# A third weights tile, two plain blocks instead of three in three of the four feed-forward layers, and earlier weight requests in sparse attention

## The chip, the cores and the metric

The kernel runs on one core of one Trainium2 chip, as one launch. The metric is the device time of that launch in microseconds (us). The median of three runs of the kernel before is 1895.46 us (1894.83 to 1896.32).

## What is computed

Two layers of a decoder on 512 tokens of width 1024, all float32. Each layer is a feed-forward part (ffn), a token mixer, and a second ffn, and every part has an RMS norm ahead of it. The mixer of the first layer is multi-head latent attention (mla, 16 heads), that of the second is native sparse attention (nsa, 16 heads in 4 groups; a compressed, a selected and a window branch with gates). So there are four ffns, numbered 0 to 3 in the code (`idx`).

```python
def swiglu(x, w_gate, w_up, w_down):
    return (jax.nn.silu(x @ w_gate) * (x @ w_up)) @ w_down
...
for i in range(DEPTH):
    h = h + 0.5 * swiglu(rmsnorm(h, ffn_norm_a[i]), ...)
    m = rmsnorm(h, mix_norm[i])
    ...
    h = h + 0.5 * swiglu(rmsnorm(h, ffn_norm_b[i]), ...)
return rmsnorm(h, final_norm)
```

The hidden width of an ffn is 2816, worked in 22 blocks of 128.

## The kernel before, in words

**Number format.** Every weight and activation is split into a high and a low part (`hi` is a rounded copy made by ScalarE, ACT; `lo` is the rest, a subtraction on VectorE, DVE, or on GpSimd, POOL). A product is three matmuls on TensorE (PE): high by high, high by low, low by high (`mm3`, L163 to L165).

**An ffn.** The residual `h` stands in eight tiles of 128 x 512. Of the 22 hidden blocks, the first three (`PLAIN`) are plain (L365 to L367): gate and up, each 8 chunks by 2 token halves by 3 matmuls of 256 columns, 96 in a block. A plain block needs only the split of `h`, chunk by chunk as the residual gets done. The other 19 blocks use Strassen's scheme with seven products (L353 to L355): 7 by 4 by 3, that is 84 matmuls of 256 columns. For that, sums of the weights (`wsums`, DVE and ACT) and sums of the activations (`combine`, made once in an ffn, for four pairs of chunks) are needed first. Besides, the blocks from the second of each three on carry `unit`s: the down projection of three finished blocks, one output chunk in each (9 matmuls of 512 columns). The last four blocks' down projection comes at the ffn's end.

**The norm's factor of ffns 1 to 3.** After the first plain block the column of sums of squares is finished (`norm_col`, four small matmuls `pc` on PE, then twelve small DVE operations, L260 to L272), then spread over the partitions by PE (`norm_bcast`, `pb`, L291) and copied to `row` by ACT. With `row` the gate of each plain block is formed (`gate`, `act`: three DVE steps of 512 columns, a Silu on ACT, and a split). Before, `pb` is written between the gate and the up half of the third plain block.

**Weight tiles.** `wslab` (L133) asks a slab of 128 x 1024 from memory (SyncE's queue) into one of two raw buffers `wr`, and splits it into a weights tile `w`. Two such tiles alternate (`wtiles`, tags w0 and w1). The plain blocks, the mixers and a part of each Strassen block (`w[1]`, `w[2]` of `wsums`, split from `rg` at L172) use them. A tile is written anew only when the matmuls that read it are done.

**Sparse attention.** `attend` goes through 96 tiles (24 in each of 4 groups): scores on PE, softmax on DVE and ACT, a scaling of the probabilities on POOL (`p`, L1091), a transpose on PE four tiles later, and the product with the values. `todo` hangs other work to tile numbers: the query, key and value projections of the next group (`make`, `vals`) and a part of the output projection (`w_o`). The first piece of each projection asks for its weights and uses them at once. While `lo_pool` is set, the low half of weights is made on POOL in two steps (L150). `compressed(g)` is done in three steps: scores, softmax (whose last step is on POOL, `e`, L1053) and `turn`, four transposes of `e` on PE (`ptc`, L1058).

**Order.** The kernel is written in program order, and the framework sets the order of each engine's queue by its own cost model and priorities. Within an engine's queue the work goes in that order, and a waiting instruction holds the ones behind it.

## Time and profile before

| | |
|---|---|
| median of the three runs | 1895.46 us |
| the profiled execution: its time | 1895.84 us |
| the profiled execution: its span | 1894.1 us |
| DVE busy | 1527.9 us (81%) |
| ACT busy | 1088.9 us (57%) |
| POOL busy | 244.7 us (13%), in the two mixers alone |
| memory | 97 GB/s mean |

How to read it: the span goes from the first to the last instruction of the profiled execution, and its own time has 1.7 us more. The ends of matmuls are modelled, so the busy time of PE overlaps itself; what a matmul costs is read from the distance between the starts of two that follow each other. The number behind the bar in a row of instructions is the time in which the engine stood idle before that group, and behind the arrow stands who ended it.

### The profile page before, as it was taken

The numbers are of one execution on the slowest core, as the hardware profiler recorded it, in microseconds if no ns is written. First come the engines' busy times: TensorE is split into PE (matmuls) and PEld (weight loads), VectorE is DVE, ScalarE is ACT, GpSimd is POOL, SyncE is SP. The second block draws the span as 40 slices with busy tenths as digits, with TensorE's granted clock in tenths as the row PEclk, the third lists the DMA queues.
The fourth block names the chain that finished last, engine by engine and source line by source line (L and its number), as shares of the span: only waits on it lengthen the run. The fifth ranks groups of instructions, "written<-read, shape, count | busy, mean of one in ns | idle before, by whom it ended". The sixth has DMA issues, their size and how long they took to land.

```text
span 1894.1 us, 32916 instructions
## 1 busy us (share of the span) xinstructions
PE 1865.5 (98%) x12504; PEld 1695.8 (90%) x12504; DVE 1527.9 (81%) x2913; ACT 1088.9 (57%) x2024; POOL 244.7 (13%) x334
## 2 busy tenths in 40 slices
PE   8999999999999999999999999999989999999998
PEld 8999999878889999998999999888778889999997
DVE  8988886677778888886898878666978988888885
ACT  8555554478765555554654555436867865555553
POOL 0000000047710000000000000015656600000000
PEclk9999999999999999999999999999999999999999
DMA  6433331311132333322333332143121133333321
GB/s 237 131 101 100 102 100 41 112 53 46 60 132 90 124 101 101 102 79 86 130 124 108 105 105 75 55 141 102 51 71 64 43 115 111 111 107 104 104 77 67
DMA packets 75902, 183.26 MB, mean 97 GB/s; under 512 B 9040, under 2 KB 37072, under 8 KB 75744
## 3 DMA queue, kind: packets, MB, share of 16 engines
q1 hardware_dynamic: 72800, 176.39, 29.4%
q10 hardware_dynamic: 2944, 4.77, 0.7%
q8 instruction: 98, 1.61, 0.4%
q14 instruction: 60, 0.49, 0.1%
HBM read 178.96 MB, written 2.16 MB: 96 GB/s over the span
## 4 chain that ended last, share of the span: by engine, by line
PE 86%; DVE 6%; ACT 4%; POOL 2%; issue 1%; DMA 0%; POOLq 0%; SPq 0%; DVEq 0%; ACTq 0%
PE pd L164 8%; PE pd L165 8%; PE pd L163 8%; PE px L353 5%; PE px L354 5%; PE px L355 5%; PE pg L353 4%; PE pg L354 4%; PE pg L355 4%; PE pq L354 3%; PE pq L353 3%; PE pq L355 3%; PE o L1139 1%; PE po L164 1%; PE po L165 1%; PE po L163 1%
## 5 line engine op out<-in xcount | busy, mean ns | idle before, releaser
L164 PE MATMUL pd<-al,wd 128*128 128x512 f32 x576 | 225.3, 391 | 0.0
L163 PE MATMUL pd<-ah,wd 128*128 128x512 f32 x576 | 224.9, 390 | 0.0
L165 PE MATMUL pd<-ah,wd 128*128 128x512 f32 x576 | 224.6, 390 | 0.0
L172 DVE TENSOR_TENSOR w<-wr,w 128x1024 fp32r<-128x1024 f32 x72 | 88.2, 1224 | 123.9 <-ACT w L171 123.9
L353 PE MATMUL px<-four,wh 128*128 128x256 f32 x608 | 168.8, 278 | 0.6 <-ACT pg L478 0.6
L355 PE MATMUL px<-four,wl 128*128 128x256 f32 x608 | 168.0, 276 | 0.0
L354 PE MATMUL px<-four,wh 128*128 128x256 f32 x608 | 167.9, 276 | 0.0
L353 PE MATMUL pq<-four,wh 128*128 128x256 f32 x608 | 167.8, 276 | 0.0
L354 PE MATMUL pq<-four,wh 128*128 128x256 f32 x608 | 167.8, 276 | 0.0
L355 PE MATMUL pq<-four,wl 128*128 128x256 f32 x608 | 167.8, 276 | 0.0
L144 ACT ACTIVATE w<-wr 128x1024 fp32r<-128x1024 f32 (+5 forms) x120 | 100.7, 845 | 113.7 <-issue 25.7
L171 ACT ACTIVATE wd<-wdr 128x384 fp32r<-128x384 f32 x192 | 99.3, 519 | 98.5 <-ACT wd L171 59.1
L402 DVE SCALAR_TENSOR_TENSOR h<-pd,h 128x512 f32<-128x512 f32 x216 | 147.9, 685 | 6.9 <-PE pd L165 6.8
L165 PEld LDWEIGHTS pd<-ah,wd 128*128 128x128 f32 x576 | 108.2, 188 | 22.8
L163 PEld LDWEIGHTS pd<-ah,wd 128*128 128x128 f32 x576 | 108.1, 188 | 20.5
L164 PEld LDWEIGHTS pd<-al,wd 128*128 128x128 f32 x576 | 108.1, 188 | 19.7
L172 DVE TENSOR_TENSOR wd<-wdr,wd 128x384 fp32r<-128x384 f32 x192 | 106.1, 555 | 16.3 <-ACT wd L171 15.6
L146 DVE TENSOR_TENSOR w<-wr,w 128x1024 fp32r<-128x1024 f32 (+4 forms) x81 | 80.7, 998 | 45.1 <-ACT w L144 44.8
L640 ACT ACTIVATE p<-p,small 128x512 f32<-128x512 f32 (+2 forms) x192 | 106.5, 557 | 17.2 <-DVE small L639 14.2
L353 PEld LDWEIGHTS px<-four,wh 128*128 128x128 f32 x608 | 114.1, 188 | 2.5 <-ACT pg L478 1.9
L353 PEld LDWEIGHTS pq<-four,wh 128*128 128x128 f32 x608 | 114.2, 188 | 0.1
L354 PEld LDWEIGHTS pq<-four,wh 128*128 128x128 f32 x608 | 114.1, 188 | 0.1
(354 smaller groups left out, 6106.3 us busy)
## 6 DMA issues: line engine op xcount, KB each, us to landing
wr<-in_w_gu SPq DMA_DIRECT2D x96, 512.0 KB, 3.3
ru<-in_w_gu SPq DMA_DIRECT2D x76, 512.0 KB, 4.2
wdr<-in_w_down SPq DMA_DIRECT2D x192, 192.0 KB, 2.4
wr<-in_w_down SPq DMA_DIRECT2D x24, 256.0 KB, 2.6
wr<-in_mla_w_o SPq DMA_DIRECT2D x8, 512.0 KB, 3.4
wr<-in_nsa_w_q SPq DMA_DIRECT2D x8, 512.0 KB, 3.3
th<-btab_d SPq DMA_DIRECT2D x16, 256.0 KB, 3.5
wr<-in_nsa_w_o SPq DMA_DIRECT2D x8, 512.0 KB, 3.6
```

The costliest lines, as they stand in the source:

```text
L144: self.copied = nc.scalar.activation(wh[:, m], raw[:, m], AF.Copy)
L146: nc.vector.tensor_tensor(wl[:, m], raw[:, m], f32v(wh[:, m]), op=ALU.subtract)
L163: mm(out, wh, xh, start=first, stop=False)
L164: mm(out, wh, xl, start=False, stop=False)
L165: return mm(out, wl, xh, start=False, stop=last)
L171: nc.scalar.activation(hi, src, AF.Copy)
L172: (nc.gpsimd if pool else nc.vector).tensor_tensor(lo, src, f32v(hi), op=ALU.subtract)
L353: mm(out, wh[:, p], xh, start=first and p == 0, stop=False, skip_group_check=True)
L354: mm(out, wh[:, p], xl, start=False, stop=False, skip_group_check=True)
L355: mm(out, wl[:, p], xh, start=False, stop=last and p == KP - 1, skip_group_check=True)
L402: nc.vector.scalar_tensor_tensor(self.h[c], p, 0.5, self.h[c], op0=ALU.mult, op1=ALU.add)
L640: nc.scalar.activation(p_sb[:, :n], p_sb[:, :n], AF.Exp, bias=nm, scale=-1.0, accum_out=sm)
```

## The change

- `PLAIN` becomes a tuple: three plain blocks in ffn 0, two in ffns 1, 2 and 3. So one more block in each of three ffns is a Strassen block. `pb` and the gates (`spread`) now stand between the gate and the up half of the last plain block, the second one in ffns 1 to 3. The sums `combine` go behind the first and the second block.
- `norm_col`'s DVE operations, and the last sums of squares ahead of them, get a higher priority (400) in ffns 1 to 3.
- `wtiles` takes turns among three tiles; the third starts with 80 unused columns, so that all tiles behind it keep their address modulo 512 bytes. 15 KB of another reservation are given up for it.
- The down projection of the last four blocks no longer uses weight tiles and `wr`, but the buffers of the Strassen sums (`fr`, `fh`, `fl`).
- In sparse attention the request for weights (`load`) is an entry of its own, one to four tiles ahead of the first piece. `turn` of groups 1 to 3 goes from 21 or 22 to 25, that is to the second tile of the next group. The scratch `t` of queries and keys gets a second buffer, and `ot` a buffer of its own.
- Latent attention: the low half of the first two queries in flight (heads 0 and 1) and of the last output go from POOL to DVE.

```diff
-PLAIN = 3
+PLAIN = 3, 2, 2, 2
...
-        t = self.first or self.wp.tile([P, 2048 + 3 * PAD], F32R, tag=f"w{self.nw % 2}", name="w")
+        shift = 5 * PAD if self.nw % 3 == 2 else 0
+        t = self.first or self.wp.tile([P, 2048 + 3 * PAD + shift], F32R, tag=f"w{self.nw % 3}", name="w")[:, shift:]
...
-        return self.rsqrt_col(pc[:, 0:4], n, pool)
+        with self.tc.high_priority(urgent) if urgent else nullcontext():
+            return self.rsqrt_col(pc[:, 0:4], n)
...
+        def spread():
+            pb = self.norm_bcast(col)
+            nc.scalar.activation(row, pb, AF.Copy)
+            for e in range(plain - 1):
+                gate(e, gates[e])
+                act(e)
...
             self.plain(idx, f, 0, g)
+            if f == plain - 1:
+                spread()
...
-            for p in (((0,), (1,), (2, 3)) if idx else ((0, 1), (2,), (3,)))[f]:
+            for p in (((0, 1), (2, 3)) if plain == 2 else ((0, 1), (2,), (3,)))[f]:
                 self.combine(p)
...
-        for f in range(PLAIN, NF):
+        for f in range(plain, NF):
...
-            down(p, self.wslab(a["w_down"][idx, c, :, tail * P :], (NF - tail, P), "act"), tail, NF)
+            raw = tp.tile([P, D], F32, tag="fr", bufs=3, name="wdr")[:, : (NF - tail) * P]
+            nc.sync.dma_start(raw, a["w_down"][idx, c, :, tail * P :])
+            w = [t[:, : (NF - tail) * P].rearrange("p (k c) -> p k c", c=P) for t in self.sum_tiles(1024)]
+            self.split(raw.rearrange("p (k c) -> p k c", c=P), *w)
+            down(p, w, tail, NF)
...
-                self.split(t, qh, ql, pool=True)
+                self.split(t, qh, ql, pool=h > 1)
...
-                    self.split(o32[0], hi, lo, pool=True)
+                    self.split(o32[0], hi, lo, pool=h + 1 < H)
...
-                return [partial(piece, k0) for k0 in range(0, KC, KC // nk)] + more
+                return [load] + [partial(piece, k0) for k0 in range(0, KC, KC // nk)] + more
...
-            make(2, (0, 1, 3, 4, 5, 6), (4, 5, 7, 8, 9, 10), (9, 10, 11, 12, 13, 14), (16, 18, 21))
-            at(2, vals(), 12, 13, 14, 15, 16, 17, 19, 20)
+            make(2, (-2, 0, 1, 3, 4, 5, 6), (2, 4, 5, 7, 8, 9, 10), (6, 9, 10, 11, 12, 13, 14), (16, 18, 25))
+            at(2, vals(), 9, 11, 12, 13, 14, 15, 16, 17, 19, 20)
```

Three places in the queues. First PE in ffn 2, before, at the norm's spread (`pb`); `pg_10244` is the gate of the third plain block.

```order
L366 MATMUL pg_10244<-x_10231,w_10504 128x256
L367 MATMUL pg_10244<-x_10231,w_10504 128x256
L365 MATMUL pg_10244<-x_10231,w_10504 128x256
L366 MATMUL pg_10244<-x_10231,w_10504 128x256
L367 MATMUL pg_10244<-x_10231,w_10504 128x256
L291 MATMUL pb_10556<-ident_79,small_76 128x128 x4
```

The same place after; `pu_10420` is the up half of the second plain block, and its lines are L368 to L370 now.

```order
L368 MATMUL pu_10420<-x_10207,w_10491 128x256
L369 MATMUL pu_10420<-x_10207,w_10491 128x256
L294 MATMUL pb_10474<-ident_79,small_76 128x128 x4
L370 MATMUL pu_10420<-x_10207,w_10491 128x256
L368 MATMUL pu_10420<-x_10233,w_10491 128x256
```

`pb` stood behind three gates and two up halves; now it stands behind two gates, one up half and 35 of the 48 matmuls of the second up half. In ffn 1 it is 21 of the 48 and in ffn 3 it is 29.

Second, DVE in ffn 2, before: the end of the norm's small operations (`small`), the weights of the last plain block (`w_10504`, `w_10584`), and the first split of the first Strassen block (`w_10674<-rg`).

```order
L146 TENSOR_TENSOR w_10504<-wr_10503,w_10504 128x1024
L271 TENSOR_TENSOR small_76<-small_76 128x4
L172 TENSOR_TENSOR wd_10810<-wdr_10811,wd_10809 128x384
L272 SCALAR_TENSOR_TENSOR small_76<-small_76 128x4
L172 TENSOR_TENSOR wd_10827<-wdr_10828,wd_10826 128x384
L146 TENSOR_TENSOR w_10584<-wr_10583,w_10584 128x1024
L172 TENSOR_TENSOR w_10674<-rg_10669,w_10674 128x1024
L378 TENSOR_TENSOR tg_10563<-pg_10242,row_10561 128x512
```

The same engine and ffn after, in two stretches: the first split of the first Strassen block (`w_10580<-rg`) among the small operations, and then their end, with the weight sums of the second Strassen block (`s1_10707`, `ru_10705`) behind it.

```order
L263 TENSOR_SCALAR small_76<-small_76 128x4
L240 TENSOR_TENSOR u_10564<-y_10563,u_10564 128x256
L264 TENSOR_SCALAR small_76<-small_76 128x4
L174 TENSOR_TENSOR w_10580<-rg_10575,w_10580 128x1024
...
L274 SCALAR_TENSOR_TENSOR small_76<-small_76 128x4
L342 TENSOR_TENSOR s1_10707<-ru_10705 128x512
L174 TENSOR_TENSOR wd_10827<-wdr_10828,wd_10826 128x384
L343 TENSOR_TENSOR ru_10705<-ru_10705,wr_10703 128x512
L174 TENSOR_TENSOR wl_10592<-rg_10575,wh_10591 128x1024
L381 TENSOR_TENSOR tg_10480<-pg_10268,row_10267 128x512
```

The split that closed the plain stage now stands in the middle of the norm's operations, and the sums of a further block begin ahead of the gates.

Third, POOL in sparse attention, before: the low half of the second value slab (`w_15658`) between the scalings `p`.

```order
L150 TENSOR_TENSOR w_15652<-wr_15651,w_15652 128x512 x2
L1091 TENSOR_SCALAR p_15508<-p_15508,small_76,gat_14124 128x512
L1091 TENSOR_SCALAR p_15532<-p_15532,small_76,gat_14124 128x512
L1091 TENSOR_SCALAR p_15564<-p_15564,small_76,gat_14124 128x384
L1091 TENSOR_SCALAR p_15604<-p_15604,small_76,gat_14124 128x384
L1091 TENSOR_SCALAR p_15626<-p_15626,small_76,gat_14124 128x256 x2
L150 TENSOR_TENSOR w_15658<-wr_15657,w_15658 128x512 x2
```

After, the second value slab is `w_15670`, and `w_16013` is the first query slab of group 3.

```order
L152 TENSOR_TENSOR w_15670<-wr_15669,w_15670 128x512 x2
L1105 TENSOR_SCALAR p_15556<-p_15556,small_76,gat_14166 128x512
L1105 TENSOR_SCALAR p_15580<-p_15580,small_76,gat_14166 128x512
L1105 TENSOR_SCALAR p_15612<-p_15612,small_76,gat_14166 128x384
L1105 TENSOR_SCALAR p_15652<-p_15652,small_76,gat_14166 128x384
L1105 TENSOR_SCALAR p_15680<-p_15680,small_76,gat_14166 128x256 x2
L152 TENSOR_TENSOR w_16013<-wr_16012,w_16013 128x512 x2
```

Each slab's low half stands one slab earlier among the same scalings.

More of the change, by code (lines that the diff above doesn't have):

```diff
@@ L49 @@
 KP = KC // 2
-PLAIN = 3
+PLAIN = 3, 2, 2, 2
 PAD = 16
+URGENT = 400
 TILES = 24
@@ L371, in ffn @@
         self.scr, self.fp = (tp, "sq", 1), tp
-        ah, al, ht, row = {}, {}, [], None
+        ah, al, ht, plain = {}, {}, [], PLAIN[idx]
         tg, tu, units = {}, {}, []
@@ L386, in act @@
             t = tu[f]
-            if f < PLAIN:
+            if f < plain:
                 t = tu_tile()
@@ L427, in ffn @@
                 tokens(t)
-        gates = [self.bank("T", "pg") for _ in range(PLAIN)]
+        def spread():
[4 more added lines that the diff above has]
+                act(e)
+        row = tp.tile([P, S], F32, tag="row", bufs=1, name="row")
+        gates = [self.bank("T", "pg") for _ in range(plain)]
         for f, g in enumerate(gates):
@@ L438, in ffn @@
                 squares(1)
-            if f == 2:
-                pb = self.norm_bcast(col)
-                row = tp.tile([P, S], F32, tag="row", bufs=1, name="row")
-                nc.scalar.activation(row, pb, AF.Copy)
-                for e in range(2):
-                    gate(e, gates[e])
-                    act(e)
             self.plain(idx, f, 1, u)
             if f == 0 and idx:
-                for c in self.late:
-                    self.sumsq(self.h[c])
-                col = self.norm_col(D, self.s2)
+                with self.tc.high_priority(URGENT):
+                    for c in self.late:
+                        self.sumsq(self.h[c])
+                col = self.norm_col(D, self.s2, URGENT)
             elif f == 1 and idx == 0:
@@ L462, in ffn @@
             nc.scalar.activation(t[:, i + 1 : i + 2], g[:, 0:1], AF.Identity, bias=t[:, i : i + 1])
-        tail = PLAIN + (NF - 2 - PLAIN) // NG * NG
-        for f in range(PLAIN, NF):
+        tail, left = (NF - 2) // NG * NG, 1
+        for f in range(plain, NF):
             if f % NG == 0 and f <= tail:
@@ L857, in pieces, with load @@
                 p, w = [], []
+                def load():
+                    w.extend(self.wslab(src, (KC, P)))
                 def piece(k0):
                     if k0 == 0:
-                        w.extend(self.wslab(src, (KC, P)))
                         p.append(self.mm_bank("pp"))
@@ L874, in done @@
                 def done(p):
-                    tt.append(qp.tile([P, S], F32, tag="t", bufs=1, name="t"))
+                    tt.append(qp.tile([P, S], F32, tag="t", bufs=2, name="t"))
                     nc.vector.tensor_tensor(tt[0], p, row, op=ALU.mult)
@@ L901, in vals, with load @@
                 ws = []
+                def load(z):
+                    ws.append(self.wslab(a["nsa_w_v"][z], (4, 256), "half"))
                 def piece(j, kk):
-                    if not ws:
-                        ws.extend(self.wslab(a["nsa_w_v"][z], (4, 256), "half") for z in range(2))
                     if kk == 0:
@@ L914, in piece @@
                         values(1, j, p)
-                return [partial(piece, j, kk) for j in range(4) for kk in range(2)]
+                return [partial(load, z) for z in range(2)] + [partial(piece, j, kk) for j in range(4) for kk in range(2)]
             def query(t2):
@@ L921, in done @@
                 def done(p):
-                    tt.append(qp.tile([P, S], F32, tag="t", bufs=1, name="t"))
+                    tt.append(qp.tile([P, S], F32, tag="t", bufs=2, name="t"))
                     nc.vector.scalar_tensor_tensor(tt[0], p, 0.125, row, op0=ALU.mult, op1=ALU.mult)
@@ L984, in nsa @@
                 kf = keys(0)
-                for f in kf[:2]:
+                for f in kf[:3]:
                     f()
@@ L991, in nsa @@
                 self.split(pk[:, : G * 32].rearrange("p (g n) -> p g n", g=G), at(kch), at(kcl))
-                for f in kf[2:]:
+                for f in kf[3:]:
                     f()
@@ L1173, in w_o, with load @@
                 w = []
+                def load():
+                    w.append(self.wslab(a["nsa_w_o"][0, c2], (2, 4, P), "act"))
                 def piece(e):
-                    if e == 0:
-                        w.append(self.wslab(a["nsa_w_o"][0, c2], (2, 4, P), "act"))
                     self.w_o1(w[0], oh[:4], ol[:4], c2 + KP * e, e, False)
-                return [partial(piece, e) for e in range(2)]
+                return [load] + [partial(piece, e) for e in range(2)]
             todo = {}
```

18 lines of the change are left out of this document (9 added, 9 removed).

## Prediction

> **What bounds the kernel now.** I read the page's busy times and chain first, then PE's waits, and then the timelines of the places that the change touches.
>
> ```profile
> PE 1865.5 (98%) x12504; PEld 1695.8 (90%) x12504; DVE 1527.9 (81%) x2913; ACT 1088.9 (57%) x2024; POOL 244.7 (13%) x334
> PE 86%; DVE 6%; ACT 4%; POOL 2%; issue 1%; DMA 0%; POOLq 0%; SPq 0%; DVEq 0%; ACTq 0%
> ```
>
> PE is busy for 98% of the span and carries 86% of the chain that ended last. So there are two ways to gain: fewer matmuls, or fewer of PE's few waits. These are the longest but for the kernel's start (engine, line, who ended it: us in total, times, longest):
>
> ```profile
> PE ptc L1058 <- POOL e L1053: 4.1, 4, 2.4
> PE pv L164 <- POOL w L150: 1.7, 2, 1.0
> PE pg L353 <- ACT pg L485: 1.2, 3, 0.8
> PE pv L163 <- ACT w L144: 0.7, 1, 0.7
> PE s L165 <- POOL four L172: 0.6, 1, 0.6
> PE po L164 <- POOL ol L172: 0.6, 1, 0.6
> PE pp L165 <- POOL w L150: 0.6, 1, 0.6
> PE px L353 <- ACT pg L478: 0.6, 3, 0.2
> ```
>
> All of them are touched by the change. I give each part its own price, as a change of the profiled execution's time of 1895.84 us (0.38 above the median of the runs shown).
>
> **A. Fewer matmuls.** Three plain blocks of 96 matmuls become Strassen blocks of 84: 36 fewer, all of 128 x 256. Their real price is the distance of starts, not the 276 ns of the page. In a steady Strassen block, the second product's first matmul and the last product's last one, 71 starts apart:
>
> ```profile
> 1131.37 0.28 PE L353 MATMUL pq<-four,wh 128*128 128x256 f32 x1
> ...
> 1139.41 0.28 PE L355 MATMUL pg<-x,wl 128*128 128x256 f32 x1
> ```
>
> That is 8.04 / 71 = 0.1133 us each, and 36 of them are **-4.1 us**. PE is the bound in this stage, so they count in full if nothing comes late.
>
> **B. The third tile at the ffns' openings.** ACT copied the first Strassen block's `rg` only when PE had released a weights tile, and DVE idled behind it in ffn 2:
>
> ```profile
> 926.95 1.06 ACT L171 ACTIVATE w<-rg 128x1024 fp32r<-128x1024 f32 x1 [4.33 <-PE pg L367]
> ```
> ```profile
> 922.65 1.23 DVE L146 TENSOR_TENSOR w<-wr,w 128x1024 fp32r<-128x1024 f32 x1 [1.44 <-ACT w L144]
> 928.04 1.22 DVE L172 TENSOR_TENSOR w<-rg,w 128x1024 fp32r<-128x1024 f32 x1 [4.16 <-ACT w L171]
> ```
>
> With a third tile these copies go ahead. PE's own waits from such late copies are those of `pg` (1.2) and `px` (0.6); between 0 and -1.8 I take **-1.0**, as new ones of the kind may come.
>
> **C. The norm's spread comes earlier than its factor.** This speaks against the change. In ffn 2 the new place of `pb` is 48 + 35 matmuls behind `pc`, which ends at 910.32:
>
> ```profile
> 909.51 0.95 PE L279 MATMUL pc<-ones,s 128*128 128x1 f32 x8
> 910.32 0.36 PE L365 MATMUL pg<-x,w 128*128 128x256 f32 x1
> ```
>
> So PE would be there at 910.32 + 83 x 0.1133 = 919.72; before, 144 matmuls stood between. DVE's twelve small operations ran from 911.30 on, with long ones in between, to the last of them:
>
> ```profile
> 905.08 0.69 DVE L237 TENSOR_TENSOR u<-y 128x512 f32<-128x512 f32 x1
> 905.68 0.42 DVE L239 TENSOR_TENSOR u<-y,u 128x256 f32<-128x256 f32 x1
> 906.02 0.42 DVE L238 TENSOR_TENSOR u<-y,u 128x256 f32<-128x256 f32 x1
> 906.35 1.22 DVE L172 TENSOR_TENSOR four<-u,four 128x1024 fp32r<-128x1024 f32 x1
> 907.49 1.22 DVE L146 TENSOR_TENSOR w<-wr,w 128x1024 fp32r<-128x1024 f32 x1
> ...
> 911.30 0.15 DVE L260 TENSOR_SCALAR small<-pc 128x4 f32<-128x4 f32 x1
> 911.37 1.21 DVE L172 TENSOR_TENSOR four<-u,four 128x1024 fp32r<-128x1024 f32 x1
> ...
> 920.59 0.15 DVE L272 SCALAR_TENSOR_TENSOR small<-small 128x4 f32<-128x4 f32 x1
> ```
>
> The rows give DVE's steps: 1.14 for 1024 columns, 0.60 for 512, 0.34 for 256, 0.07 for a small one. In the new order five of 1024, four of 512 and two of 256 stand between the twelve: 5.7 + 2.4 + 0.68 + 0.84 = 9.6, an end at 920.9, and PE waits 1.2. In ffns 1 and 3 the same sum starts from
>
> ```profile
> 572.59 0.36 PE L365 MATMUL pg<-x,w 128*128 128x256 f32 x1
> 1554.76 0.36 PE L365 MATMUL pg<-x,w 128*128 128x256 f32 x1
> ```
> ```profile
> 572.95 0.16 DVE L260 TENSOR_SCALAR small<-pc 128x4 f32<-128x4 f32 x1
> 1555.28 0.15 DVE L260 TENSOR_SCALAR small<-pc 128x4 f32<-128x4 f32 x1
> ```
>
> with 69 and 77 matmuls ahead of `pb` (PE there at 580.41 and 1563.48) and 8.0 and 8.8 us of DVE order (ffn 1: three of 1024, four each of 512 and 256; ffn 3: four, four, three): ends at 580.97 and 1564.10, waits of 0.6 and 0.6. Together **+2.4**. Behind the waiting `pb` stand the rest of the up half and the whole Strassen block, so PE pays each wait in full. The bounds are 0, if DVE gets there a little sooner, and 5, if each is some 0.8 later.
>
> Is the rest of DVE's work in time? In ffn 2 its new order from the last residual add to the low half of the block's second sums (needed by the third product) has sixteen operations of about 512 columns, nine of 1024, eight of 256 and twelve small: 9.6 + 10.3 + 2.7 + 0.8 = 23.4.
>
> ```profile
> 899.27 0.68 DVE L402 SCALAR_TENSOR_TENSOR h<-pd,h 128x512 f32<-128x512 f32 x1
> ```
>
> From 899.27 that is 922.7. PE begins the block at 910.32 + 96 x 0.1133 + 0.8 (`pb`) + 1.2 = 923.2 and its third product 24 matmuls later, at 925.9: 3.2 us to spare. I cost it at nothing, and the cover is these 3.2 us.
>
> **D. `turn` four tiles later.** The four waits on `e` sum to 4.1; that of group 0 stays, at 0.36. The longest one:
>
> ```profile
> 1315.00 0.33 PE L1058 MATMUL ptc<-ident,e 128*128 128x128 f32 x1 [0.36 <-POOL e L1053]
> 1411.34 0.66 PE L1058 MATMUL ptc<-ident,e 128*128 128x128 f32 x4 [2.38 <-POOL e L1053]
> ```
>
> At most -3.7. The turned tile is first read at the group's tile 10 (the first end, 3, and the lead and lag of 4 and 3), so at tile 1 it is still in time.
>
> **E. Weights asked early.** `pv` and `pp` waited 1.7 + 0.7 + 0.6 = 3.0 for slabs. And just behind the `pv` waits, PE's granted clock fell (window, length, PE, PEld, DVE, ACT, POOL busy, then PEclk):
>
> ```profile
> 1382.00:1387.00 5.00, 2.54 (x14) 1.90 (x13) 3.90 (x12) 4.09 (x10) 4.26 (x5) 0.91 0.05 17
> 1387.00:1389.00 2.00, 2.00 (x11) 2.00 (x11) 1.28 (x7) 0.42 (x2) 1.37 (x2) 0.50 0.78 262
> 1389.00:1395.00 6.00, 6.00 (x44) 5.58 (x44) 2.43 (x14) 3.08 (x12) 1.46 (x4) 0.96 0.01 3
> ```
>
> 5 x 0.09 + 2 x 0.50 + 6 x 0.04 = 1.7 us of clock lost, right after the stretch in which PE was busy for 2.54 of 5 us. I count it to the same waits: at most -4.7. [...] After the wait of 2.38 us the clock did not fall (the 0.99 of the 120 us below is this one fall, 1.7 of 120), so the trace does not settle it.
>
> The request passes SyncE's table loads, ACT's exponentials and POOL's scalings by one to four tiles, and on POOL it holds them for
>
> ```profile
> 1371.44 2.58 POOL L150 TENSOR_TENSOR w<-wr,w 128x512 fp32r<-128x512 f32 x2
> ```
>
> 2.58 us, as it did in its old place; the probabilities have a lead of four tiles to cover it. I add nothing.
>
> D and E make -8.4 at most. I take three quarters, **-6.3**: in that stage DVE is busy for 98.81 of 120 us, and a softmax that is behind can take a freed wait over.
>
> ```profile
> 1300.00:1420.00 120.00, 112.68 (x647) 94.17 (x646) 98.81 (x318) 93.69 (x235) 78.04 (x105) 0.99 0.24 74
> ```
>
> **F. Latent attention's three low halves on DVE.** PE's waits for POOL there are 0.6 (`s`) and 0.6 (`po`); a 512-column step of DVE takes 0.60. **-1.0** (0 to -1.2). The ffns' last down weights keep their operations and only change buffers: 0.
>
> **G. Matmuls that read the third tile.** No row shows it. The nearest are the two products that read weights tiles:
>
> ```profile
> L354 PE MATMUL px<-x,w 128*128 128x256 f32 x304 | 85.3, 281 | 0.0
> L354 PE MATMUL pg<-x,w 128*128 128x256 f32 x304 | 83.9, 276 | 0.0
> ```
>
> 24 of a block's 84 matmuls read such a tile, in 79 blocks every third time the new one: 632, and 5 ns each way are 3.2 us. Its address is the same modulo 512 as the others', so I take **0**.
>
> **Sum.** -4.1 - 1.0 + 2.4 - 6.3 - 1.0 + 0 = -10.0 against 1895.84, so 1885.8, and 1885.5 on the scale of the median.
>
> **Rivals.**
> - *All goes well*: no new wait and every old one gone, -4.1 - 1.8 - 8.4 - 1.2 = -15.5: 1880.0. For it: `pb`'s lateness is under a microsecond in two ffns. Against: DVE's load in sparse attention. 0.13.
> - *The clock falls anyway*, as a mechanism of its own: three quarters of 1.7 stay: 1886.8. 0.10.
> - *The waits only move*, that is, the early requests don't do what they say, because there are still two raw buffers and one POOL queue, and the softmax takes the waits over: A, B and C alone, -2.7: 1892.8. For it: POOL 78.04 and DVE 98.81 of 120 us. Against: the low halves stand one slab earlier in POOL's queue. 0.13.
> - *Slower: DVE becomes the bound of the openings.* If DVE ends the first Strassen split no sooner than before (928.04 + 1.22 = 929.26), PE, there at 923.2, waits 6.1 in each of three ffns: +18.2, and -10.0 + 18.2 = +8.2: 1903.7. It decides from 3.3 us an ffn. For it: DVE was busy for 27.40 of 33 us there. Against: the new order has that split among the norm's operations, and the tile it needs is free. 0.06.
>
> ```profile
> 900.00:933.00 33.00, 33.00 (x294) 33.00 (x293) 27.40 (x51) 19.20 (x27) 0.00 (x0) 1.00 0.47 158
> ```
>
> **How the numbers follow.** The forecast has 0.58. Within 0.2% of 1895.46 (3.8 us, about what a measurement of this kernel tells from no change) lie most of the "waits only move" case: same 0.10. Slower 0.06, faster 0.84. The range reaches from the best case, 1880.0, up to 1891.5; left out are most of "waits only move" and the slower case, 0.19 together. It holds C's bounds (1883.1 to 1888.1), and D, E together from the full gain to about 0.
>
> **What would show it.** In the profile after: 36 fewer matmuls; PE's waits for `e` down to about 0.4 and for `w` in sparse attention gone; no clock of 0.50 near the value projection; a wait of `pb` for `small` of about 1 us in each of ffns 1 to 3; no idle of DVE behind `w<-rg`. I am wrong if PE waits several us at the first or second Strassen block, or if the sparse attention stage is no shorter.

## The result, and the profile after

The changed kernel takes 1883.27 us (median of four runs, 1882.53 to 1884.34), the kernel before 1895.74 us on the same chip: a ratio of 0.9935, 95% interval 0.9918 to 0.9952. The prediction was 1885.5 us. The profiled execution after has a span of 1882.5 us and a time of 1884.34 us, 11.5 us less than the one before.

The page after: busy times, and the chain that ended last.

```profile
PE 1859.2 (99%) x12468; PEld 1691.9 (90%) x12468; DVE 1550.1 (82%) x2940; ACT 1080.1 (57%) x2039; POOL 243.2 (13%) x331
PE 85%; DVE 7%; ACT 4%; DMA 2%; issue 1%; POOL 0%; SPq 0%; DVEq 0%; ACTq 0%; POOLq 0%
```

The 36 matmuls are gone (12504 to 12468). PE's waits after (us in total, times, longest):

```profile
PE pb L294 <- DVE small L274: 1.9, 4, 0.9
PE s L165 <- DVE small L650: 1.6, 4, 0.7
PE px L356 <- ACT pg L485: 1.1, 3, 0.5
PE pg L356 <- ACT pg L492: 0.6, 3, 0.3
PE s L167 <- DVE four L174: 0.5, 1, 0.5
PE ptc L1072 <- POOL e L1067: 0.4, 1, 0.4
```

All waits for `w` in sparse attention are gone, and `ptc` is down from 4.1 to 0.4. New or longer are `pb` (0.2 before) and, in mla, `s` for DVE's `small` (0.2 before) and `four` (0.6 for POOL's before). `px` and `pg` together are 1.7, as against 1.8 before: they have moved, not gone.

Where did the time come from? Both traces are cut at PE's first matmul of each stage. Lengths in us:

| stage | before | after | difference |
|---|---|---|---|
| ffn 0 | 340.39 | 340.75 | +0.36 |
| mla | 214.72 | 214.96 | +0.24 |
| ffn 1 | 337.66 | 337.63 | -0.03 |
| ffn 2 | 337.32 | 337.45 | +0.13 |
| nsa | 307.23 | 297.31 | -9.91 |
| ffn 3 | 342.91 | 340.62 | -2.29 |

So sparse attention gave nearly all, and ffns 1 and 2 gave nothing although each lost 12 matmuls. The order of ffn 0 is the same in after and in e2, e3, e5, e7, e8 and e11 below, and its length went from 340.57 to 343.64 us over these executions, so no difference under 3 us is read from that stage. Ffns 1 and 2 have the same order in after, e2, e3 and e5 and took 336.88 to 337.68 and 336.87 to 337.76 us, so that tenths there are read from waits, not from lengths.

The stretch of sparse attention whose row the prediction showed, after (length, then PE, PEld, DVE, ACT, POOL busy, PEclk):

```profile
1300.00:1420.00 120.00, 118.51 (x692) 99.73 (x691) 105.33 (x345) 100.52 (x256) 83.84 (x114) 1.00 0.24 77
```

PE is busy for 118.51 us of 120, where it was 112.68, and the clock is full throughout. DVE went from 98.81 to 105.33 and did not become the bound.

What took the gain of ffns 1 and 2? First the new `pb`. The timeline after, DVE, in ffn 1:

```profile
573.36 0.16 DVE L262 TENSOR_SCALAR small<-pc 128x4 f32<-128x4 f32 x1 [0.52 <-PE pc L281]
...
575.33 1.22 DVE L174 TENSOR_TENSOR w<-rg,w 128x1024 fp32r<-128x1024 f32 x1
576.47 0.16 DVE L274 SCALAR_TENSOR_TENSOR small<-small 128x4 f32<-128x4 f32 x1
...
581.38 0.15 DVE L274 SCALAR_TENSOR_TENSOR small<-small 128x4 f32<-128x4 f32 x1
```

Twelve small operations of 0.16 us take 8.2 us, because the order puts up to 1.22 us of other work between each two. PE waits 0.40, 0.36 and 0.24 us for the last of them in ffns 1 to 3. Second, waits in the middle of the ffns. ACT, after, at a place of ffn 1:

```profile
856.34 1.06 ACT L146 ACTIVATE w<-wr 128x1024 fp32r<-128x1024 f32 x1 [2.47 <-DMA wr<-in_w_gu]
857.31 0.36 ACT L492 ACTIVATE pg<-px 128x256 f32<-128x256 f32 x1
```

A weights tile is free, so ACT's queue has come to the copy of the next slab; but there are only two raw buffers, the slab is still on its way, and ACT stands for 2.47 us with the product's copy behind it. PE waits 0.20 us for that copy. With 0.16 us more for each matmul that starts again after a wait (this one stands 0.47 us behind the one before it, 0.20 of that the wait, where others of its kind are 0.11 apart), 12 matmuls less and the waits that went and came make -0.3 us in ffn 1, -0.4 in ffn 2 and -2.6 in ffn 3. Measured are 0.0, +0.1 and -2.3, so 0.3 to 0.5 us in each stay unexplained.

The groups of ACT's copies of `rg` slabs show the same for the whole kernel (busy us, mean ns, then the idle time ahead of them and who ended it), before and after:

```profile
L171 ACT ACTIVATE w<-wr 128x1024 fp32r<-128x1024 f32 x72 | 76.5, 1062 | 60.5 <-PE pg L355 58.8 <-DMA wr<-in_w_gu 1.7
```
```profile
L173 ACT ACTIVATE w<-wr 128x1024 fp32r<-128x1024 f32 x75 | 78.7, 1049 | 6.9 <-DMA wr<-in_w_gu 6.6 <-PE pg L370 0.2
```

Before, ACT waited 58.8 us for PE to release a tile and 1.7 for the DMA. After, the wait for PE is gone and that for the DMA is 6.6.

In mla, `pb` (the query norm's) waits 0.91 us where it was 0.24. All engines, after:

```profile
396.16 1.03 POOL L152 TENSOR_TENSOR w<-wr,w 128x384 fp32r<-128x384 f32 x1 [6.16 <-ACT w L146]
...
396.33 0.87 DVE L272 SCALAR_TENSOR_TENSOR small<-small 128x4 f32<-128x4 f32 x1
...
397.75 0.46 PE L294 MATMUL pb<-ident,small 128*128 128x128 f32 x2 [0.91 <-DVE small L274]
```

One small operation takes 0.87 us, its neighbours 0.16, and it ends (397.20) when POOL's subtraction ends (397.19). With a third tile this slab is split earlier than before, beside the norm (with two tiles, in e1, no small operation is stretched, and `pb` waits 0.27 us).

### The profile page after: what moved, and what is told of

Read it like the earlier page. It is cut to its first block, busy times and chain, and to the rows that moved or that the text cites. A ratio compares the mean times of both kernels' runs of the same rounds, so it can differ in the third digit from the quotient of the medians.

```text
span 1882.5 us, 32808 instructions
## 1 busy us (share of the span) xinstructions
PE 1859.2 (99%) x12468; PEld 1691.9 (90%) x12468; DVE 1550.1 (82%) x2940; ACT 1080.1 (57%) x2039; POOL 243.2 (13%) x331
## 4 chain that ended last, share of the span: by engine, by line
PE 85%; DVE 7%; ACT 4%; DMA 2%; issue 1%; POOL 0%; SPq 0%; DVEq 0%; ACTq 0%; POOLq 0%
PE pd L166 8%; PE pd L165 8%; PE pd L167 8%; PE px L356 5%; PE px L357 5%; PE px L358 5%; PE pg L356 4%; PE pg L357 4%; PE pg L358 4%; PE pq L357 3%; PE pq L358 3%; PE pq L356 3%; PE o L1153 2%; PE pt L1128 2%; PE po L165 2%; PE po L167 2%
## 5 line engine op out<-in xcount | busy, mean ns | idle before, releaser
L356 PE MATMUL px<-four,wh 128*128 128x256 f32 x632 | 175.4, 278 | 1.2 <-ACT pg L485 1.1
L357 PE MATMUL px<-four,wh 128*128 128x256 f32 x632 | 174.6, 276 | 0.0
L358 PE MATMUL pq<-four,wl 128*128 128x256 f32 x632 | 174.4, 276 | 0.0
L356 PE MATMUL pq<-four,wh 128*128 128x256 f32 x632 | 174.4, 276 | 0.0
L357 PE MATMUL pq<-four,wh 128*128 128x256 f32 x632 | 174.4, 276 | 0.0
L174 DVE TENSOR_TENSOR wl<-s,wh 128x512 fp32r<-128x512 f32 x79 | 54.5, 690 | 123.0 <-ACT wh L173 122.9
L146 ACT ACTIVATE w<-wr 128x1024 fp32r<-128x1024 f32 (+5 forms) x90 | 79.2, 888 | 87.0 <-PE po L167 17.5
L173 ACT ACTIVATE wh<-s 128x512 fp32r<-128x512 f32 x79 | 49.8, 630 | 134.5 <-PE px L357 131.0
L356 PEld LDWEIGHTS px<-four,wh 128*128 128x128 f32 x632 | 118.6, 188 | 2.6 <-ACT pg L485 2.4
L358 PEld LDWEIGHTS pq<-four,wl 128*128 128x128 f32 x632 | 118.7, 188 | 0.0
L357 PEld LDWEIGHTS px<-four,wh 128*128 128x128 f32 x632 | 118.7, 188 | 0.0
L358 PEld LDWEIGHTS px<-four,wl 128*128 128x128 f32 x632 | 118.6, 188 | 0.0
L356 PEld LDWEIGHTS pq<-four,wh 128*128 128x128 f32 x632 | 118.6, 188 | 0.0
```

The costliest lines, as they stand in the source:

```text
L146: self.copied = nc.scalar.activation(wh[:, m], raw[:, m], AF.Copy)
L173: nc.scalar.activation(hi, src, AF.Copy)
L174: (nc.gpsimd if pool else nc.vector).tensor_tensor(lo, src, f32v(hi), op=ALU.subtract)
L356: mm(out, wh[:, p], xh, start=first and p == 0, stop=False, skip_group_check=True)
L357: mm(out, wh[:, p], xl, start=False, stop=False, skip_group_check=True)
L358: mm(out, wl[:, p], xh, start=False, stop=last and p == KP - 1, skip_group_check=True)
```

## The experiments

Labels e1 to e4 ran beside the kernel before at 1895.83 us, e5 to e8 at 1897.06, e9 to e11 at 1896.54, e12 at 1897.23. e5 is the changed kernel once more, and e3 turned out to be it too: their medians and that of the first measurement are 1884.07, 1886.04 and 1883.27 us. So the experiments are read from stages and waits, and not from medians that lie 1 or 2 us apart.

**e1: two weights tiles.**

```diff
-        shift = 5 * PAD if self.nw % 3 == 2 else 0
+        shift = 0
...tag=f"w{self.nw % 2}"
```

> The changed kernel with two weights tiles that alternate, as before, and all else as changed. If the third tile carries the change: the first Strassen split in ffns 1 to 3 again waits for a tile, and the slabs asked early in sparse attention wait for one too, so PE waits 1 to 6 us in each of ffns 1 to 3 and some of the 3 us of slab waits come back in sparse attention: 1887 to 1903 us. If the order of the queues does it all and the tile is only room: within 1.5 us of the changed kernel's 1883.3.

1889.68 us, ratio 0.9965 (0.9952 to 0.9978); sparse attention 301.86 us, 4.55 longer than after. PE's waits:

```profile
PE pv L166 <- POOL w L152: 1.5, 2, 1.1
PE pv L165 <- ACT w L146: 0.6, 1, 0.6
PE pp L167 <- POOL w L152: 0.5, 1, 0.5
```

The slab waits are back, and so is the clock of 0.50 for 3.41 us behind them. The code still asks early, but the queue does not. SyncE's request of the first value slab, in e1:

```profile
1337.95 0.35 SPq L143 DMA_DIRECT2D wr<-in_nsa_w_v  x1
```

That is 103.0 us after the stage's first matmul; it was 103.4 in before and is 86.3 in after. So the early request itself comes from the third tile.

The other half of the expectation failed: the first Strassen split in ffns 1 to 3 waits for no tile here either. ACT in ffn 2, with two tiles:

```profile
915.78 1.06 ACT L173 ACTIVATE w<-rg 128x1024 fp32r<-128x1024 f32 x1
```

Before, ACT stood idle for 4.33 us ahead of the same copy. So that idle time went by the rest of the change, not by the third tile; by which part of it, the runs do not tell. PE still waits 1.46 us for `px` at 588.98 in ffn 1 and 1.14 for `pg` at 1583.82 in ffn 3, and ffns 1 to 3 are 1.3 us longer together than after. At its copies of `rg` slabs ACT waits 62.2 us for PE and 3.0 for the DMA, about as before. Mla is 1.41 us shorter than after.

**e2: `turn` back at tiles 21, 21 and 22.**

```diff
-make(1, ..., (16, 18, 25)); make(2, ..., (16, 18, 25)); make(3, ..., (16, 18, 25))
+make(1, ..., (16, 18, 21)); make(2, ..., (16, 18, 21)); make(3, ..., (16, 18, 22))
```

> The changed kernel with the turn of groups 1 to 3 back at tiles 21, 21 and 22. If those three waits for e were worth what the trace of before showed (3.7 us, and about 0.2 more at each restart): the sparse attention stage goes from 297.3 to about 301 us and the time to 1886.5 to 1888. If the softmax takes a freed wait over, as my three quarters allowed for: 1884.5 to 1886. If it was never worth anything: 1883.3.

1888.21 us, ratio 0.9959 (0.9945 to 0.9974); sparse attention 302.19 us, 4.88 longer.

```profile
PE ptc L1072 <- POOL e L1067: 3.2, 3, 2.4
```

The waits for `e` are back, and again the clock falls, to 0.50 from 1405.52 to 1408.93, now behind a single wait of 2.37 us. So in e1 and e2 it fell behind whichever waits were left.

**e3: slabs asked at the first piece's tile**, the other two parts as changed.

```diff
-            make(2, (-2, 0, 1, 3, 4, 5, 6), (2, 4, 5, 7, 8, 9, 10), (6, 9, 10, 11, 12, 13, 14), (16, 18, 25))
+            make(2, (0, 0, 1, 3, 4, 5, 6), (4, 4, 5, 7, 8, 9, 10), (9, 9, 10, 11, 12, 13, 14), (16, 18, 25))
```

(and so in the five other lines of this kind)

> The changed kernel with each slab of sparse attention asked at the tile of its first piece again (turn stays late, three tiles stay). If the early requests are worth what the waits of before showed: PE waits about 3 us for w (lines pv and pp) and the clock may fall again next to them, 3 to 5 us longer: 1886.3 to 1888.3. If the clock fell for another reason than these waits: the 3 us come back without a clock of 0.5. If the third tile alone takes these waits away: within 1 us of 1883.3.

1886.04 us (1883.86 to 1886.97), ratio 0.9944 (0.9929 to 0.9959); sparse attention 297.42 us, 0.11 from after, no clock fall. But the edit did not reach the chip. PE's, DVE's, ACT's and POOL's instructions stand in the same order in both traces, and SyncE asks for the slabs at the same times. The first value slab, in after and then in e3:

```profile
1322.82 0.33 SPq L143 DMA_DIRECT2D wr<-in_nsa_w_v  x1
```
```profile
1324.03 0.33 SPq L143 DMA_DIRECT2D wr<-in_nsa_w_v  x1
```

Counted from the stage's first matmul (1236.53 and 1237.72) that is 86.29 and 86.31 us, though the edit moved this request by three tiles. So e3 is the changed kernel a third time, and with e1 it says what the entries `load` do: nothing. With two tiles the request is late though the code asks early, with three it is early though the code asks late. Its ffn 0 is 1.6 us longer than in after, with a wait of `px` of 1.60 us where after has 0.52.

**e4: three plain blocks in all ffns**, the rest as changed.

```diff
-PLAIN = 3, 2, 2, 2
+PLAIN = 3, 3, 3, 3
```

> The changed kernel with three plain blocks in all four ffns. If fewer matmuls count in full: 36 more matmuls, +4.1 us, less the waits of pb (1.0 us in ffns 1 to 3), which has more time then: ffns 1 to 3 together 3 us longer, 1886.3. If ffns 1 and 2 got nothing from the fewer matmuls because DVE or ACT sets their pace: at most 1 us longer, or shorter.

1889.03 us, ratio 0.9954 (0.9940 to 0.9969). Sparse attention 297.32, as after. Ffns 1 to 3 are 0.44, 1.69 and 0.70 us longer than after, 2.8 together, where 36 matmuls are 4.1: the three `pb` waits are gone. The rest came from a stage that the edit doesn't touch: mla is 2.4 us longer, with the queues of after. POOL and DVE there, and PE:

```profile
395.81 1.02 POOL L152 TENSOR_TENSOR w<-wr,w 128x384 fp32r<-128x384 f32 x1 [6.28 <-ACT w L146]
395.85 0.98 DVE L272 SCALAR_TENSOR_TENSOR small<-small 128x4 f32<-128x4 f32 x1
...
397.04 0.99 POOL L152 TENSOR_TENSOR w<-wr,w 128x384 fp32r<-128x384 f32 x1 [0.22 <-DVE small L273]
397.07 0.98 DVE L274 SCALAR_TENSOR_TENSOR small<-small 128x4 f32<-128x4 f32 x1
...
398.19 0.57 PE L294 MATMUL pb<-ident,small 128*128 128x128 f32 x3 [1.83 <-DVE small L274]
```

Two small operations meet a subtraction of POOL here, not one. `pb` waits 1.83 us, and the clock falls to 0.50 for 3.41 us right behind it (from 398.67). In after, e2, e3 and e5 one operation meets it, here and in e8 two, all with the same queues: that is chance from one execution to the next.

**e5: the changed kernel once more.**

> The changed kernel once more, unaltered, beside three variants of it on one chip, so that tenths of a microsecond can be read between them. Expected by every theory: 1882.5 to 1884.3 us, with the same waits as before: PE for pb in the middle of feed-forwards 1 to 3 (0.40, 0.36, 0.24 us) and in MLA (0.91), PE for a product's copy by ACT (rows px and pg, 1.1 and 0.6 us in all).

1884.07 us (1883.48 to 1884.20), ratio 0.9930 (0.9915 to 0.9944), the same waits but for one of `px` in ffn 2, which is not there.

**e6: a third raw buffer.**

```diff
-        raw = self.wp.tile([P, 1024], F32, tag="wr", bufs=2, name="wr")
+        raw = self.wp.tile([P, 1024], F32, tag="wr", bufs=3, name="wr")
```

(and so at the two other places of this tag)

> The changed kernel with a third raw buffer wr (the weights as the DMA brings them) beside its third weights tile. Theory (the third weights tile lets ACT's copy of a slab be queued as soon as the tile is free, but with two raw buffers the slab's DMA isn't back by then, so ACT stands in its queue on the DMA, 2.54 us ahead of the copy of L492 at 304.7 us and 0.81 us ahead of that of L485 at 643 us, and PE waits for the product's copy behind it): the PE rows px<-L485 and pg<-L492, 1.1 + 0.6 us of waits and 2.9 us with the restarts, fall to under 1 us with the restarts, and the time by 1.5 to 2.5 us against the changed kernel on the same chip. Rival (those copies are late because ACT's order has other ready work in front of them, whatever the raw buffers): the waits stay at 1 us or more with another distribution, and the time is within 0.7 us of the changed kernel.

1884.32 us, ratio 0.9931 (0.9916 to 0.9946): the time of e5, where the theory had 1.5 to 2.5 us less. In ffns 1 and 2 the theory held: not one `px` or `pg` wait is left, lengths 336.31 and 336.39 us against 337.68 and 337.21 in e5. The group of ACT's copies of `rg` slabs in e6:

```profile
L173 ACT ACTIVATE w<-wr 128x1024 fp32r<-128x1024 f32 x75 | 79.6, 1062 | 57.9 <-PE pg L358 56.9 <-DMA wr<-in_w_gu 0.8 <-PE pg L370 0.2
```

The slab is there in time (0.8 us of waits for the DMA instead of 6.6), and ACT waits for PE's release of the tile again. The gain of 2.2 us is lost elsewhere: mla 215.78 (+0.87, `pb` 1.78 us, two meetings with POOL), ffn 0 342.14 (+1.05), ffn 3 +0.5. PE's rows:

```profile
PE pb L294 <- DVE small L274: 2.8, 4, 1.8
...
PE px L356 <- ACT pg L485: 1.4, 1, 1.4
...
PE pq L356 <- DVE tu L392: 0.5, 1, 0.5
```

The longest `px` and the `pq` are in ffn 0 (48.16 and 44.88 us), where the order of ACT is another one with three buffers. It is not shown that the third buffer brought these losses: e8 has two meetings and a `pb` of 1.79 us in mla with two buffers, and e3, e7 and e11 have a `px` of 1.6 us at this place of ffn 0 with the order of after. Only the wait of `pq` is new.

**e7: two query slabs of mla behind the query norm's row.**

```diff
-                return self.wslab(a["mla_w_q"][h], (3, P), "act")
+                with self.tc.issue_after(self.row_copy.ins) if h in (3, 4) else nullcontext():
+                    return self.wslab(a["mla_w_q"][h], (3, P), "act")
```

(`row_copy` is ACT's copy of `pb`)

> The changed kernel, but in MLA ACT's copies of the query slabs of heads 3 and 4 are queued behind its copy of the query norm's broadcast row, so that POOL's low halves of these two slabs come after the twelve small instructions of the norm's column and not beside them. Theory (one of those small instructions on DVE, L272 at 396.33 us, took 0.87 us where its neighbours took 0.16, because POOL's subtraction of the head-3 slab ran from 396.16 to 397.19, and pb waited 0.91 us for the column): every small instruction of this column takes 0.16 to 0.17 us, PE's wait for pb in MLA falls from 0.91 to 0.2 or 0.3 us (0.24 before the change, where POOL was idle there), and MLA is some 0.7 us shorter, if the slabs are still in time for heads 3 and 4. Rival (the column is late because of DVE's other work between its instructions, and the long one is a record's accident): the wait stays above 0.7 us and MLA's length within 0.3 us. A mishap that would show as a wait of pq or s for w: the slabs come too late, and MLA is longer by 1 us or more.

1882.99 us (1881.14 to 1883.26), ratio 0.9921 (0.9905 to 0.9938): each run under each run of e5, if by less than the changed kernel's own medians differ. Mla is 213.25 us, 1.66 shorter than in e5 (after, e2, e3 and e5 are within 0.1 us of each other there). DVE:

```profile
397.28 0.16 DVE L272 SCALAR_TENSOR_TENSOR small<-small 128x4 f32<-128x4 f32 x1
...
397.87 0.16 DVE L272 SCALAR_TENSOR_TENSOR small<-small 128x4 f32<-128x4 f32 x1
```

No small operation is stretched, POOL's first subtraction starts at 400.88, and `pb` waits 0.19 us. The theory held. The other 0.9 us of mla are waits further on that went with it (`s` for `four` is gone).

**e8: `pb` behind the up half of the last plain block in ffns 1 to 3.**

```diff
             self.plain(idx, f, 1, u)
+            if f == plain - 1 and idx:
+                spread()
```

> The changed kernel, but in feed-forwards 1 to 3 the norm's broadcast pb and what follows it (the row, gate and act of block 0) are asked for behind the second plain block's up half instead of between its gate and up halves, some 8 us of PE later. Theory (the new wait of pb is only for the norm's column, which DVE makes in 8.2 us because it puts 0.4 to 1.2 us of other work between the twelve small instructions): the three waits (0.40, 0.36, 0.24 us; 1.5 us with the restarts) go, nothing takes their place, and the time falls by 1.0 to 1.6 us. Rival (the gates are wanted early: the products after them take T banks that the two gates hold, and the activations of blocks 0 and 1 pile up on DVE and ACT behind the row): PE waits for px, pg or a T bank at the start of the products by 0.5 us or more in each of the three, and the time is the same within 0.5 us or up to 3 us longer.

1883.29 us, ratio 0.9925 (0.9910 to 0.9940), 0.8 us from e5 with touching ranges. Ffns 1 to 3 are 337.59, 337.34 and 340.17 us against 337.68, 337.21 and 340.04: no gain. The three `pb` waits are gone, and in their place stand

```profile
PE px L356 <- ACT pg L487: 1.1, 4, 0.4
PE pg L356 <- ACT pg L494: 0.7, 3, 0.4
...
PE px L356 <- ACT uq L491: 0.5, 2, 0.2
```

`px` for ACT right behind the plain blocks (0.24 us at 591.86, 0.09 at 926.43, 0.16 and 0.23 at 1560.69 and 1564.00). Both sides were half right: the wait goes, and about as much comes back right behind it. That it is the lateness of the gates which gives it back, as the rival had it, is read from the place of these waits and was not tested by itself. Mla, which the edit doesn't touch, is 215.64 us here, with two meetings and a `pb` of 1.79.

**e9: e6 and e7 together.** The two diffs above.

> The changed kernel with both additions that removed waits by themselves: a third raw buffer (took the waits px and pg out of feed-forwards 1 and 2, 1.3 and 0.8 us of their lengths, but came with 1.1 us more in feed-forward 0 and 0.9 in MLA) and the query slabs of heads 3 and 4 behind the query norm's row (MLA 1.7 us shorter). Theory (the two act in different places, and the 0.9 us that the third raw buffer cost in MLA was POOL's subtraction beside two of the norm's small instructions instead of one, which the later slabs take away): feed-forwards 1 and 2 at 336.3 us, MLA at 213 to 213.5, feed-forward 0 at 341 to 342, and 2.5 to 4 us less than the changed kernel, a ratio to the kernel before of 0.9910 to 0.9920. Rival (a wait that goes in one place only comes back in the next, since ACT and DVE are in arrears there by the same amount): the sum of PE's waits in feed-forwards and MLA stays within 1 us of the changed kernel's, and so does the time, ratio 0.993 or above.

1883.17 us (1881.83 to 1883.85), ratio 0.9929 (0.9915 to 0.9943): no better than e7 alone, and the 2.5 to 4 us of the theory did not come. Ffns 1 and 2 are 336.27 and 336.43 as expected; but mla is 214.51, with `pb` at 0.20 us but `s` waits for `four` (0.47) and for `small` (0.69) back, and ffn 0 has the two waits of e6 again (1.44 and 0.53).

**e10: no padding of the third tile.**

```diff
-        shift = 5 * PAD if self.nw % 3 == 2 else 0
+        shift = 0
```

> The changed kernel without the padding of the third weights tile (shift of 0 instead of 80 columns), so that this tile is 8384 bytes long and every later tile of its pool lies at another address by 512; the order of the instructions on every engine is the same. Prediction's term (the padding costs and gives nothing by itself, term G): 1883.3 to 1884.3 us, ratio 0.993 to 0.9935, no group of matmuls with another mean. Rival (addresses by 512 matter to TensorE's reading of the moving operand or to an engine's writing, as the care for them in the kernel suggests): some groups of matmuls or of DVE's and ACT's instructions get longer by a per cent or more, and the time rises by 2 us or more.

1910.37 us, ratio 1.0073 (1.0059 to 1.0087), with the same order on every engine, no new wait, and a mean clock of 0.999. The products, first in after, then in e10 (busy us, mean ns):

```profile
L357 PE MATMUL px<-four,wh 128*128 128x256 f32 x632 | 174.6, 276 | 0.0
...
L357 PE MATMUL px<-x,w 128*128 128x256 f32 x316 | 88.6, 280 | 0.0
...
L357 PE MATMUL pg<-x,w 128*128 128x256 f32 x316 | 87.2, 276 | 0.0
```
```profile
L357 PE MATMUL px<-four,wh 128*128 128x256 f32 x632 | 177.8, 281 | 0.0
...
L357 PE MATMUL pg<-x,w 128*128 128x256 f32 x316 | 88.4, 280 | 0.0
```

The products that read `four` are 4 to 6 ns longer by their rows, and those of `pg` of `x` by 3 to 5; `px` of `x` and `w` is not (280 and 279). With six groups of 632 and six of 316 of that kind, 5688 matmuls by 4 to 5 ns are 23 to 28 us, which is about all of the loss (26.3 us against e5). The rival held, and by far.

**e11: mla's low halves back on POOL.**

```diff
-                self.split(t, qh, ql, pool=h > 1)
+                self.split(t, qh, ql, pool=True)
...
-                    self.split(o32[0], hi, lo, pool=h + 1 < H)
+                    self.split(o32[0], hi, lo, pool=True)
```

> The changed kernel with MLA's low halves back on POOL (the two places where the change moved those of heads 0 and 1 and of the last pair to DVE). Prediction's term F (the move takes 1.0 us off, the waits of s for POOL's four, 0.63 us, and of po for POOL's ol, 0.63 us): MLA is 1 us longer than in the changed kernel, with these two waits back, and the time rises by 1 us. Rival (what the move took from POOL came back on DVE, s for DVE's four 0.50 us and s for DVE's small at 406.6 us 0.67 us, so that it gave nothing): MLA within 0.4 us, the time the same.

1888.52 us (1885.24 to 1890.85), ratio 0.9957 (0.9941 to 0.9973). Mla is 217.70 us, 2.79 longer than in e5 (the profiled execution lost 2.6 more in ffn 0, which the edit doesn't touch). PE waits for `four` for 2.20 us, where the wait was 0.63 in the kernel before, and the clock falls to 0.50 behind it (409.84 to 413.25); `po` waits 0.62 us for `ol` again. POOL:

```profile
404.82 2.52 POOL L152 TENSOR_TENSOR w<-wr,w 128x512 fp32r<-128x512 f32 x2 [3.19 <-ACT w L146]
407.30 1.26 POOL L174 TENSOR_TENSOR four<-tq,four 128x512 fp32r<-128x512 f32 x1
```

With the third tile POOL's 2.52 us for a value slab stand just ahead of the query's low half; before, they stood behind it.

**e12: the padding behind the third tile's data**, so that only this tile's own address by 512 is another one.

```diff
-..., name="w")[:, shift:]
+..., name="w")
```

> The changed kernel with the 80 columns of padding behind the third weights tile's data and not ahead of them: later tiles keep their addresses by 512, but the third tile itself lies at another address by 512 than the first two; the order of instructions is the same. Without any padding the products that read four and the sum tiles wh took 281 to 283 ns by the page instead of 276 to 278, and the time was some 26 us longer. Theory 1 (what costs is where the moving operand and the tiles behind the weights pool lie, so the padding works through the later tiles alone): the time of the changed kernel, ratio 0.992 to 0.994, and those products at 276 to 278 ns. Theory 2 (the weights tile's own address counts, as the prediction's term G weighed it: 632 matmuls of 5 ns): the groups that read w, px and pg of x and w, get 1 to 2 ns longer in the mean, and the time rises by 2 to 4 us, ratio 0.994 to 0.996. Both at once would be 0.995 with the products of four unchanged.

1888.13 us (1887.04 to 1888.32), ratio 0.9946 (0.9932 to 0.9959), a span of 1885.2 against 1882.2 in e5. The products that read `w` are 2 ns longer in the mean, those of `four` at most 1:

```profile
L357 PE MATMUL px<-four,wh 128*128 128x256 f32 x632 | 175.0, 277 | 0.0
...
L357 PE MATMUL px<-x,w 128*128 128x256 f32 x316 | 89.0, 282 | 0.0
...
L357 PE MATMUL pg<-x,w 128*128 128x256 f32 x316 | 88.0, 278 | 0.0
```

Theory 2 held for the tile itself, and e10 showed the same for the tiles behind it.

## Why the prediction was right

The time came out 2.2 us under the forecast and inside its range, by errors of opposite sign: sparse attention gave 3.6 us more than D and E had, everything else 2.1 less (-1.6 instead of -3.7). That makes 1.5; the other 0.7 is how far the two profiled executions lie from their medians. So the number is in part luck: A and G came as forecast, D and E had the right waits at too low a price, and B and F gave nothing.

**A** (-4.1): right as far as the runs can tell. e4 shows it from the other side: ffns 1 to 3 are 2.8 us longer, which is 4.1 us of matmuls less 1.3 for the `pb` waits (1.5 with the restarts).

**B** (-1.0): wrong, the measure is 0. "With a third tile these copies go ahead" has the wrong cause: ACT's copy of `rg` in ffn 2 stands at 910.50 us with no idle ahead of it, but with two tiles it does so too (e1, 915.78). And I took PE's old waits as a cover that can only shrink. The step that failed is "between 0 and -1.8": with two raw buffers a free tile sent ACT into waiting for a DMA, with the products' copies behind it, and 1.7 us came back. ACT's waits for the DMA show the cause: 3.0 us with two tiles (e1), 6.6 with three, 0.8 with a third raw buffer (e6).

**C** (+2.4): mis-sized. The waits were 0.40, 0.36, 0.24 us, 1.0 in all, and 1.5 by the distance of starts, since PE's first matmul behind a wait took about 0.16 more. Counted from the start of each ffn, DVE's end came within 0.1 us of my sum in ffns 1 and 3 and 0.6 us sooner in ffn 2, and PE was at `pb` 0.2 to 0.3 us later than I had it. What I did not have is the fourth `pb`, in mla: a norm whose code does not change, hit by POOL's earlier slab (e7, and e1, where it is not).

**D and E** (-6.3, at most -8.4): right in mechanism, too small. The full gain came, 9.9 us by the length of the stage: the 3.7 and 3.0 us of waits, 1.5 more for the restarts behind them (8.2 by the distance of starts), 1.6 of clock, and 0.1. The step that failed is "I take three quarters": DVE at 98.81 of 120 us had room, for it went to 105.33 and nobody waited more. The request ahead of time, which the step names as the cause, did come, at 86.3 us of the stage instead of 103.4, but by the third tile and not by the new entries: with two tiles it is at 103.0 though the code asks early (e1), with three at 86.3 though it asks late (e3).

**F** (-1.0): wrong as a gain. The two waits went, but `s` for DVE's `four` and `small` took their place (0.49 and 0.67 us), and with the later `pb` mla is 0.24 us longer. Yet e11 shows the edit to be needed: the price of leaving it out was 2.8 us, the fall of the clock among them, as the third tile had changed what stands ahead of it on POOL. I had priced it against the old order.

**G** (0): right, and the address was the right thing to look at; that 512 bytes is the step that counts was an assumption, which no run shows. Had it been another, e12 gives what I had estimated (632 matmuls by 5 ns, 3.2 us; measured 3.0 by the spans of e12 and e5). That the same holds for all tiles behind it, with some nine times the matmuls, I had not seen.

**The rivals.** *The clock falls anyway*: it did not, but e1, e2, e4 and e11 each brought the fall back with a wait. *The waits only move*: not in sparse attention; in ffns 1 and 2 and in mla, yes. *DVE becomes the bound of the openings*: PE's longest wait there is 0.40 us, not 6.1. *All goes well* failed on B, C and F.

## What to carry to other kernels

One more buffer in a chain can send the engines on to the next scarce thing (here ACT from 58.8 us of waits for PE to 6.6 for the DMA): count the raw buffers behind the split tiles, and look at what each in-order queue will stand on, and whom that puts next to whom. Price every part of a change against the order that the other parts make, not against the old one: here a move of three subtractions gained nothing by itself and kept 2.8 us from being lost. And a new tile is also a shift of all tiles behind it, which can cost more than the tile brings (here 1910.37 us without the padding, with 1896.54 for the kernel before). Last, look at the queues that an edit makes before reading its time: the early requests of this change are early by the tile alone, and the late ones of e3 were not late.

## What the runs showed of the hardware

**The falls of the clock lay on a grid of 3.413 us in these runs.** The trace's clock records have 1.00 for 1375.571 us, 0.50 for 3.413 and 1.00 for 501.759 in before, and 1.00 for 1867.090 us in after: 403, 147 and 547 times 3.4133 us. In e1, e2, e4 and e11 a window of 3.41 or 3.42 us is at 0.50, and the one ahead of it at 1.00. Windows cut on that grid show how much of PE's work stood ahead of a fall, which the prediction left open. In e2, and in e8 (window, length, PE busy ..., PEclk):

```profile
1402.10:1405.52 3.42, 1.05 (x9) 0.79 (x8) 2.81 (x9) 2.43 (x8) 3.42 (x5) 1.00 0.28 65
1405.52:1408.93 3.41, 3.41 (x15) 3.04 (x14) 1.80 (x4) 1.66 (x3) 1.10 (x2) 0.50 0.39 137
```
```profile
396.31:399.72 3.41, 1.62 (x12) 1.23 (x11) 2.15 (x4) 0.52 (x1) 2.01 (x2) 1.00 0.42 128
399.72:403.13 3.41, 3.41 (x18) 2.60 (x16) 2.02 (x4) 2.25 (x4) 0.51 (x1) 1.00 0.29 94
```

And in before, first around its fall, then around the wait of 2.38 us that had none:

```profile
1382.67:1386.09 3.42, 1.36 (x7) 0.95 (x7) 2.35 (x8) 2.66 (x5) 3.39 (x4) 1.00 0.00 1
1386.09:1389.50 3.41, 3.09 (x13) 3.06 (x14) 2.20 (x9) 1.68 (x7) 1.85 (x3) 0.50 0.47 156
...
1406.57:1409.98 3.41, 2.40 (x19) 2.00 (x17) 3.34 (x13) 3.41 (x10) 3.41 (x4) 1.00 0.00 0
1409.98:1413.39 3.41, 2.05 (x15) 1.92 (x16) 2.09 (x7) 1.69 (x5) 2.82 (x4) 1.00 0.46 154
```

The wait of 2.38 us lay across a border: PE was busy for 2.40 and 2.05 us in the two windows, and the clock stayed at 1.00. A window with PE busy for 1.05 (e2), 1.23 (e11), 1.36 (before), 1.58 (e4) or 1.74 us (e1) was followed by one at 0.50; with 1.62 (e8) and 1.72 us (e6) it was not, nor near the kernel's end with 1.54 (before, 1884.43 to 1887.85). So the clock fell behind each of these three windows with at most 1.36 us of work, by one wait (e2) or by several (before), and between 1.54 and 1.74 us it went either way; what decides there is not shown. In the fall of before, matmuls of 256 columns started 0.213 us apart, where it was 0.118 ahead of it; from the first start inside it (1386.41) to the first behind it (1389.54) are 3.13 us, so that I estimate its cost at 1.4 to 1.6 us.

**Small DVE operations ended with a POOL subtraction.** In mla they took 0.87 (after, 396.33) and twice 0.98 us (e4, 395.85 and 397.07) instead of 0.16. Each started 0.03 to 0.17 us behind the start of POOL's subtraction and ended within 0.02 us of its end. One that started 0.09 us ahead of the subtraction took 0.16 us (before, 396.96, POOL from 397.05), and in e7, where POOL's first subtraction starts at 400.88, none of them takes more than 0.17. By what means POOL's instruction does this, the runs do not show.

**Matmuls of 256 columns took longer when weights tiles moved.** With the same order and no new wait, `px` of `four` and `wh` (L357) took 276 ns in after, 113.6 from start to start, and 281 ns in e10. The padded tile is 8704 bytes long; without the padding it is 8384, and the tiles behind it lie 320 bytes lower. That the address by 512 is what matters fits this, but 256 or 128 would fit as well, and no run tells them apart. In kernel.py the pools of `x` and `four` stand ahead of that of the weights tiles, so neither of them moved: for the products of `four` only the weights did, the Strassen sums `wh` and `wl`. In e12, too, it was only weights, with 2 to 3 ns more for `pg` of `x` and `w` (276 and 278 to 279 ns), a third of whose matmuls read that tile. The 512-column matmuls of the down projection, whose tiles moved as far in e10, took 390 ns as in after. Why `px` of `x` and `w` was no slower in e10 (280 and 279 ns), the runs do not settle.
